# One PSUM product ahead of the second context transpose, 56 unread products ahead of the first inverse, one weight cast bound in the merge

## The chip, the cores and the metric

The kernel runs on one core of a Trainium2 chip. The metric is the time of one execution on the device, in microseconds (us). The engines are TensorE (PE in the rows, PEld for its weight loads), VectorE (DVE), ScalarE (ACT), GpSimd (POOL) and SyncE (SP), whose queue issues most DMAs.

## What is computed

One layer of a hybrid network over 512 latent tokens and 256 context tokens of width 1024, batch 1, in fp32. Cut to what matters here:

```
x   = ffn(x);  ctx = ffn(ctx)                       # half-step SwiGLU blocks with adaLN modulation
qa, ka, va, qkv, z, a, b, ga, gb = split(modulate(x)   @ w_in)   # and the same for ctx
o_a = neighbourhood_attention(qa, ka, va, ctx keys)
q, k, v = silu(conv(qkv)) ...                       # gated delta rule, 4 heads, two directions
per chunk:  T = inverse(I + tril(k k^T * decay * beta));  scan over chunks
o_b = rmsnorm(scan output) * silu(z)
y   = sigmoid(ga) * (o_a @ w_pa) + sigmoid(gb) * (o_b @ w_pb)    # the merge
x   = LN(alpha*x + gate * (y @ w_o));  x = ffn(x)
```

## The kernel before

**Products.** Every weight is cast into two fp32r parts, a rounded one (`wh`, on ScalarE) and the rest (`wl`, on VectorE), in `split`, and so is every activation (`uxh`, `uxl` for the latent tokens, `uch`, `ucl` for the context). A product of 128 weights by 512 tokens is three matmuls for each of 8 slices of the depth (`mm3k`, lines 190 to 192). A `Stream` loads weights by DMA (line 172) and casts them one or two tiles ahead of their use, into a few rotating buffers.

**Order.** The instructions of the whole program are put in order on each engine when the program is built, by a planner: it times them by its own estimates and takes, among those that it holds ready, the one that stands first in the code. On the chip each engine works through its queue in that order, and waits where an input is late. `tc.issue_after(x)` holds an instruction behind `x` in the queue of their engine.

**PSUM.** PSUM has eight banks of 128x512 fp32. The up and down products of the first block use the pool `pp` with one tag `ps` of eight tiles, handed out in rotation. The last users of that pool are the four `z` products, the transposes of the context tokens in `u2(fc, pp, "c", 0, ...)`, the first product of `units[0]` (the query of head 0) and the transposes of `u2(fc, pp, "c", 1, ...)`. A call of `u2` takes two tiles: TensorE writes four 128x128 transposes into each (line 146), ScalarE reads them into `u` (line 149), and `split` makes `uch` and `ucl` of that. Then the pool is closed, and its banks go to the pools `pm` (three tiles for products) and `pg` (five for transposes). The first tile of `pm` is the key product of head 0.

**Gram stage, inverse and scan.** The delta rule is done in three batches `bi` of chunks. `grams(bi)` loads the decays (`Dt<-gcd`), makes the Gram products (`pq`, line 857), scales them on VectorE (`Bt`, line 927, `At`, line 931) and stores them (`bd<-Bt`); `base_inverse` loads 32x32 diagonal blocks back (`Ltr`, `L`), inverts them row by row on VectorE (lines 954, 955) and stores them (`rd<-Xt`). `inverse` loads these (`T<-rd`, line 976), transposes them on VectorE (lines 978, 979), and joins them with small products into the tag `pi`, each read by VectorE or ScalarE before the next. `scan_step` uses the tag `pc` of two tiles. Behind each of these small products `turn` lets some pieces of the other projections (`fill_spill`, 6 matmuls each, tag `pm`) run on TensorE. The code says `step(grams(0))`, which includes the base inverse of the first batch, `base = grams(1)`, then `inv_of(0, 0)`, `step(base, 4)` and so on: the second base inverse on VectorE lies beside the first two inverses.

**Merge.** For each of 8 tiles `m` the loop fills the stream `wso` of `w_o` weights, makes the product with `w_pa` from the stream `ws` (`gated`), multiplies it by the gate (line 1333, VectorE), adds it to `yb` (line 1334, GpSimd) and splits the sum into `yh`, `yl`. The gates are loaded (`gt<-gad`) into two buffers. `wso` items 4 to 6 have buffers in a pool that opens right ahead of this loop. After it come the products with `w_o`, and in `finish2` the residual `xr<-x1d`, loaded from GpSimd's queue into memory that the merge has used, and a layer norm for each of four token tiles.

Of the kernel before, what the change touches and what calls it, by code (L numbers as in the profile page):

```python
# [10 lines left out]
F32 = mybir.dt.float32  # L11
F32R = mybir.dt.float32r
AF = mybir.ActivationFunctionType
ALU = mybir.AluOpType
# [4 lines left out]
P = 128  # L19
# [39 lines left out]
def body(ctx, tc, I, out, dbg=None):  # L59
    nc = tc.nc  # L60
    V, S, G, T = nc.vector, nc.scalar, nc.gpsimd, nc.tensor
    dbg = dbg or {}

    def pool(name, side="left", space=None):
        kw = dict(name=name, bufs=1, reuse_waits="tile")
        if space is not None:
            kw["space"] = space
        else:
            kw["side"] = side
        g = tc.tile_pool(**kw)  # L70
        st = ExitStack()
        p = st.enter_context(g)
        return p, st.close
# [3 lines left out]
    def tl(p, shape, tag, bufs=1, dt=F32):  # L77
        uid[0] += 1
        return p.tile(list(shape), dt, name=f"{tag}_{uid[0]}", tag=tag, bufs=bufs)
# [22 lines left out]
    marks = {}  # L102
# [29 lines left out]
    def split(src, hi, lo, behind=()):  # L132

        with tc.issue_after(behind[0]) if behind else nullcontext():
            S.copy(hi, src)  # L135
        with tc.issue_after(behind[1]) if behind else nullcontext():
            V.tensor_tensor(lo, src, hi.bitcast(F32), ALU.subtract)  # L137

    def to_u(tp, pp, xn, uh, ul, c0, scale, shift, tag="u32"):

        u32 = tl(tp, [P, KT, P], tag)
        for hb in range(2):
            ps = tl(pp, [P, 4, P], "ps", 8)
            for q in range(4):
                k = hb * 4 + q
                T.transpose(ps[:, q, :], xn[:, k * P:(k + 1) * P], ident)
            for q in range(4):
                k = hb * 4 + q
                S.activation(u32[:, k, :], ps[:, q, :], AF.Identity, bias=shift[:, k:k + 1], scale=scale[:, k:k + 1])
            ks = slice(hb * 4, hb * 4 + 4)  # L150
            split(u32[:, ks], uh[:, ks, c0:c0 + P], ul[:, ks, c0:c0 + P])
        return u32

    class Stream:
# [7 lines left out]
        def fill(self, n):  # L162
            while len(self.q) < n and self.i < len(self.srcs):
                src, p, bufs, rp, rb = self.srcs[self.i], self.wp, self.bufs, self.wp, self.bufs
                if isinstance(src, tuple):
                    if src[1] not in self.extra:
                        return
                    p, bufs, rp, rb = self.extra[src[1]]
                    src = src[0]
                c = src.shape[-1]  # L170
                raw = self.raw() if self.raw else tl(rp, [P, D], "wr", rb)
                nc.sync.dma_start(raw[:, 0:c], src)
                hi = tl(p, [P, D], "wh", bufs, F32R)
                lo = tl(p, [P, D], "wl", bufs, F32R)
                split(raw[:, 0:c], hi[:, 0:c], lo[:, 0:c], self.behind.get(self.i, ()))
                self.q.append((hi, lo))
                self.i += 1

# [9 lines left out]
    def mm3k(ps, wh, wl, uh, ul, k, nk=KT):  # L188
        a, b = wh[:, k * P:k * P + P], wl[:, k * P:k * P + P]
        T.matmul(ps, a, uh[:, k, :], start=(k == 0), stop=False)  # L190
        T.matmul(ps, a, ul[:, k, :], start=False, stop=False)  # L191
        T.matmul(ps, b, uh[:, k, :], start=False, stop=(k == nk - 1))  # L192

    def down(pp, ws, hs, ntt, kl, pre=(), between=None, after=None, pieces=0, post=(), n=None):

# [115 lines left out]
    def secs(col, s):  # L311
        return col[:, s * 8:s * 8 + 8]
# [7 lines left out]
    def raw1():  # L320
        raws[0] += 1
        k = raws[0] % (5 if more[0] else 3)
        return tl(more[0], [P, D], "wr", 2) if k > 2 else tl(wx, [P, D], "wr") if k == 0 else tl(wp, [P, D], "wr", WB)
# [5 lines left out]
    uxh = tl(up, [P, KT, NX], "uxh", 1, F32R)  # L329
# [35 lines left out]
    def order1():  # L365
        t = lambda fs: [I["up1"][2 * f + j] for f in fs for j in range(2)]
        dn = lambda a, b: rows(I["dn1"], range(a, b))
        o = t(range(F0, F1)) + t(range(F1)) + t(range(F1, HF)) + dn(0, HF) + dn(0, HF - 2)
        o += t(range(HF, NF)) + dn(HF, NF - 4)
        n = len(o)  # L370
        o += dn(HF, NF - KL1)
        o = [(w, "x") if j % 3 == 2 else w for j, w in enumerate(o)]
        return o[:n] + [(w, "tail") for w in dn(NF - 4, NF)] + o[n:]
# [56 lines left out]
    pp, close_pp = pool("pp1", space=PSUM)  # L430
    ws = Stream(wp, order1(), WB, 1)
# [3 lines left out]
    for t in range(2):  # L435
        raw = raw1()
# [76 lines left out]
    def u2(p, pp, kind, t, y):  # L513
        uh, ul, col = (uxh, uxl, colx) if kind == "x" else (uch, ucl, colc)
        to_u(p, pp, y, uh, ul, t * P, secs(col, 4), secs(col, 3))
# [8 lines left out]
    uxh = tl(ux, [P, KT, NX], "uxh", 1, F32R)  # L524
# [31 lines left out]
    src = [I["wab"] if n == "ab" else I["w" + n][m] if n in ("pa", "pb") else I["win"][WIN_IDX[(n, m)]] for n, m in order]  # L556
# [18 lines left out]
    ws = ws2  # L575
    names = iter(order)

    def win_w(name, m):
        assert next(names) == (name, m)
        return ws.get()  # L580
# [240 lines left out]
        units += [decay()] * (h == 2) + [unit_q(h), unit_k(h), unit_v(h), unit_kc(h), unit_vc(h)]  # L821
    u2(fc, pp, "c", 0, ys[0])
    next(units[0])
    u2(fc, pp, "c", 1, ys[1])
    close_fc()
    close_pp()
# [18 lines left out]
    pgq, close_pgq = pool("pgb", space=PSUM)  # L845
# [68 lines left out]
    def gram(p, s, bd, g):  # L914

        mats = mats_of(s)
        Dt = tl(gb_, [P, 4, P], "Dt", 2)
        nc.sync.dma_start(Dt[:], bass.AP(gcd.tensor, gcd.offset + (4 * s + 2 * p) * P, [[0, P], [24 * P, 2], [1, 2 * P]]))
        for m, (d, c, i) in enumerate(mats):
            msk = cst[:, (C_MF if d == 0 else C_MB):][:, 0:P]  # L920
            V.scalar_tensor_tensor(Dt[:, m], Dt[:, m], gcum[:, d, s, 2 * p + i:2 * p + i + 1], msk, op0=ALU.subtract, op1=ALU.add)
        S.activation(Dt[:], Dt[:], AF.Exp)
        Bt, At = tl(gq, [P, 4, P], "Bt", NBT), None
        for n, t in enumerate(products(p, s)):
            if n == 0:
                for m, (d, c, i) in enumerate(mats):
                    V.scalar_tensor_tensor(Bt[:, m], t[m] if s == 1 else t[:, m], beta[:, d, s, 2 * p + i:2 * p + i + 1], Dt[:, m], op0=ALU.mult, op1=ALU.mult)
                nc.sync.dma_start(bass.AP(bd.tensor, bd.offset + g * MSTR, [[P, P], [4 * MSTR, 4], [1, P]]), Bt[:])
            else:
                At = tl(gq, [P, 4, P], "At", NAT)  # L930
                V.tensor_tensor(At[:], t[:], Dt[:], ALU.mult)
        return Bt, At
# [190 lines left out]
    def grams(bi):  # L1123
        bd = tl(dp, [16 * MSTR], f"bd{bi}")[:]
        rds[bi] = tl(dp, [64, 1024], f"rd{bi}")[:]
        for j in (0, 2, 1, 3) if bi == 0 else range(4):
            res[(bi, j)] = gram(j % 2, 2 * bi + j // 2, bd, 2 * (j % 2) + j // 2)
        return base_inverse(bd, rds[bi])

    def step(gen, n=8):  # L1130
        for _ in range(n):
            next(gen, None)

    def inv_of(bi, st):
        inv[(bi, 2 * st)], inv[(bi, 2 * st + 1)] = inverse(bi, st, rds[bi], [res[(bi, 2 * st + p)][0] for p in range(2)])
# [6 lines left out]
        next(fills)  # L1142
    step(grams(0))
    base = grams(1)
    inv_of(0, 0)
    step(base, 4)
    inv_of(0, 1)
# [134 lines left out]
    def gated(name, gd, m, oh, ol):  # L1282
        wh, wl = win_w(name, m)
        gt = tl(np_, [P, NX], "gt", 2)
        nc.sync.dma_start(gt[:], gd[m])
        ps = tl(pm, [P, NX], *PMB)
        mm3(ps[:], wh, wl, oh, ol, 4)
        return gt, ps
# [15 lines left out]
    for m in range(4):  # L1304
        if m == 3:
# [5 lines left out]
            wso = Stream(wp, [(w, k) if k else w for w, k in zip(rows(I["w_o"], range(KT)), ("b", "b", "b", "b", "o", "o", "o", ""))], WB, 1)  # L1311
# [18 lines left out]
    for m in range(8):  # L1330
        wso.fill(min(4 + (m + 1) // 2, 7))
        gt, ps = gated("pa", gad, m, oah, oal)
        V.scalar_tensor_tensor(gt[:], gt[:], 1.0, ps[:], op0=ALU.add, op1=ALU.mult)
        G.tensor_tensor(yb[:, m], yb[:, m], gt[:], ALU.add)
        split(yb[:, m], yh[:, m], yl[:, m])
# [4 lines left out]
    pp, close_pp = pool("pp3", space=PSUM)  # L1340
# [4 lines left out]
    uxh = tl(up, [P, KT, NX], "uxh", 1, F32R)  # L1345
# [70 lines left out]
    src = [I["up2"][i] for i in range(2 * NH)]  # L1416
    ws = Stream(wp, [(w, key(j)) if key(j) else w for j, w in enumerate(src)], WB, 2)
# [134 lines left out]
    ws = Stream(wp, [(w, "d") if j % 6 > 1 else w for j, w in enumerate(rows(I["dn2"], range(NF)))], WB, 2)  # L1552
    ws.extra = {"d": (wd, 4, wp, WB)}
    raw = hs[NH:]
# [7 lines left out]
    banks, _ = down(pp, ws, hs, 4, KL2, between=between, pieces=PIECES, n=NF)  # L1562
    for t in range(4):
        h = tl(lp, [P, D], "h4", 2)
        n, m = (512, D) if t < 3 else (D // PIECES, 512)
# [125 lines left out]
```

## Time and profile before

| | |
|---|---|
| runs without a profile | 1529.4, 1525.82, 1529.38 us; median 1529.38 us |
| the profiled execution | 1530.66 us, span of its instructions 1528.8 us |
| mean granted TensorE clock | 0.988 of full speed |
| instructions | 23646, of them 9221 matmuls |

A timeline row reads: start, duration, engine, line, operation, output<-inputs, shapes, count, and in brackets the idle time of the engine just ahead of it and what ended that. Matmuls are pipelined: the duration of one is longer than the distance to the next start, and it is the distance that is paid. A row of windows gives for a stretch its length, then the busy time of each engine with the count of instructions, the granted TensorE clock, the share of DMA and GB/s.

### The profile page before, as it was taken

The numbers are of one execution on the slowest core, as the hardware profiler recorded it, in microseconds if no ns is written. First come the engines' busy times: TensorE is split into PE (matmuls) and PEld (weight loads), VectorE is DVE, ScalarE is ACT, GpSimd is POOL, SyncE is SP. The second block draws the span as 40 slices with busy tenths as digits, with TensorE's granted clock in tenths as the row PEclk, the third lists the DMA queues.
The fourth block names the chain that finished last, engine by engine and source line by source line (L and its number), as shares of the span: only waits on it lengthen the run. The fifth ranks groups of instructions, "written<-read, shape, count | busy, mean of one in ns | idle before, by whom it ended". The sixth has DMA issues, their size and how long they took to land.

```text
span 1528.8 us, 23646 instructions
## 1 busy us (share of the span) xinstructions
PE 1462.6 (96%) x9221; PEld 1258.7 (82%) x9221; DVE 1050.0 (69%) x1792; ACT 605.4 (40%) x1005; POOL 226.8 (15%) x224
## 2 busy tenths in 40 slices
PE   6999999999999999999996899999999999999997
PEld 4779988888888887889875778867678999998886
DVE  8765942597554587768777895576669699886426
ACT  5444221322222255546543444266416444344310
POOL 0000000000000011323301001366421022220001
PEclk9999999999999999999998999999999999999999
DMA  9665742667454334222476634283353143333422
GB/s 370 207 237 180 222 142 97 211 213 260 168 192 146 130 112 137 87 90 79 141 216 180 172 99 122 69 284 117 91 174 138 56 139 102 106 110 139 138 83 83
DMA packets 107586, 230.72 MB, mean 151 GB/s; under 512 B 34177, under 2 KB 47825, under 8 KB 107473
## 3 DMA queue, kind: packets, MB, share of 16 engines
q1 hardware_dynamic: 105312, 221.79, 44.7%
q10 hardware_dynamic: 1586, 5.32, 0.9%
q0 software_dynamic: 576, 2.10, 0.4%
q8 instruction: 72, 1.18, 0.3%
q14 instruction: 40, 0.33, 0.1%
HBM read 206.33 MB, written 22.85 MB: 150 GB/s over the span
## 4 chain that ended last, share of the span: by engine, by line
PE 76%; DVE 10%; DMA 7%; issue 3%; ACT 2%; POOL 2%; SPq 0%; DVEq 0%; ACTq 0%; POOLq 0%
PE ps L209 19%; PE ps L190 8%; PE ps L192 8%; PE ps L191 8%; PE pm L190 5%; PE pm L192 5%; PE pm L191 5%; PE pc L857 2%; PE ps L1478 2%; PE ps L1480 2%; PE ps L1479 2%; DVE wl L137 2%; PE po L1266 1%; DMA T<-rd 1%; PE pt L1255 1%
## 5 line engine op out<-in xcount | busy, mean ns | idle before, releaser
L137 DVE TENSOR_TENSOR wl<-wr,wh 128x1024 fp32r<-128x1024 f32 (+1 forms) x215 | 263.0, 1228 | 195.1 <-ACT wh L135 194.3
L135 ACT CAST wh<-wr 128x1024 fp32r<-128x1024 f32 (+1 forms) x215 | 217.8, 1018 | 333.4 <-PE ps L209 105.0
L192 PE MATMUL ps<-uxh,wl 128*128 128x512 f32 (+1 forms) x496 | 179.6, 363 | 2.2 <-DVE wl L137 2.2
L191 PE MATMUL ps<-uxl,wh 128*128 128x512 f32 (+1 forms) x496 | 179.3, 363 | 0.8 <-DVE uxl L137 0.8
L190 PE MATMUL ps<-uxh,wh 128*128 128x512 f32 (+1 forms) x496 | 179.6, 365 | 0.0
L279 DVE SCALAR_TENSOR_TENSOR adap<-wr,crow 128x1024 f32<-128x1024 f32 x112 | 136.8, 1221 | 38.5 <-DMA wr<-in_w_adaT_dram 37.1
L112 POOL TENSOR_TENSOR rs<-ve,mhalf 128x1 f32<-128x1 f32 (+2 forms) x46 | 50.4, 1099 | 744.6 <-DVE ve L108 735.4
L190 PE MATMUL pm<-uxh,wh 128*128 128x512 f32 x320 | 133.0, 416 | 4.1 <-ACT spill L609 2.1
L192 PE MATMUL pm<-uxh,wl 128*128 128x512 f32 x320 | 128.2, 401 | 0.7 <-DVE wl L137 0.7
L191 PE MATMUL pm<-uxl,wh 128*128 128x512 f32 x320 | 127.8, 399 | 0.0
L192 PEld LDWEIGHTS ps<-uxh,wl 128*128 128x128 f32 x496 | 93.7, 189 | 17.9 <-DVE wl L137 3.3
L191 PEld LDWEIGHTS ps<-uxl,wh 128*128 128x128 f32 x496 | 94.0, 189 | 14.9 <-DVE uxl L137 1.0
L190 PEld LDWEIGHTS ps<-uxh,wh 128*128 128x128 f32 x496 | 93.4, 189 | 14.3 <-issue 0.8
L190 PE MATMUL ps<-uch,wh 128*128 128x256 f32 x352 | 98.6, 280 | 0.0
L192 PE MATMUL ps<-uch,wl 128*128 128x256 f32 x352 | 98.3, 279 | 0.0
L191 PE MATMUL ps<-ucl,wh 128*128 128x256 f32 x352 | 98.2, 279 | 0.0
L209 PE MATMUL ps<-wh,hx 128*128 128x512 f32 x352 | 94.8, 389 | 0.0
L209 PEld LDWEIGHTS ps<-wh,hx 128*128 128x128 f32 x352 | 65.9, 188 | 13.6
L190 PEld LDWEIGHTS pm<-uxh,wh 128*128 128x128 f32 x320 | 61.6, 193 | 16.3 <-ACT spill L609 3.0
L192 PEld LDWEIGHTS pm<-uxh,wl 128*128 128x128 f32 x320 | 61.7, 193 | 14.8 <-DVE wl L137 1.5
L191 PEld LDWEIGHTS pm<-uxl,wh 128*128 128x128 f32 x320 | 61.6, 192 | 10.6
L190 PEld LDWEIGHTS ps<-uch,wh 128*128 128x128 f32 x352 | 66.1, 188 | 0.6
(411 smaller groups left out, 3438.7 us busy)
## 6 DMA issues: line engine op xcount, KB each, us to landing
wr<-in_w_adaT_dram SPq DMA_DIRECT2D x88, 512.0 KB, 4.7
wr<-in_up_dram SPq DMA_DIRECT2D x80, 512.0 KB, 4.2
wr<-in_dn_dram SPq DMA_DIRECT2D x58, 512.0 KB, 3.5
wr<-in_win_dram SPq DMA_DIRECT2D x52, 512.0 KB, 3.9
rb<-in_up_dram SPq DMA_DIRECT2D x18, 512.0 KB, 3.7
wr<-in_w_o_dram SPq DMA_DIRECT2D x8, 512.0 KB, 4.0
ac<-in_up_dram SPq DMA_DIRECT2D x6, 512.0 KB, 5.2
Dt<-gcd SPq DMA_DIRECT2D x12, 256.0 KB, 5.1
```

Of the source, the lines that this page charges most:

```text
L112: G.tensor_tensor(rs[:], ve[:], mhalf[:, 0:n], ALU.pow)
L135: S.copy(hi, src)
L137: V.tensor_tensor(lo, src, hi.bitcast(F32), ALU.subtract)
L190: T.matmul(ps, a, uh[:, k, :], start=(k == 0), stop=False)
L191: T.matmul(ps, a, ul[:, k, :], start=False, stop=False)
L192: T.matmul(ps, b, uh[:, k, :], start=False, stop=(k == nk - 1))
L209: T.matmul(banks[t][d][:, c0:c1], a[:, sl], b[:, d * 512 + c0:d * 512 + c1], start=first and j == 0, stop=last and j == 2)
L279: V.scalar_tensor_tensor(pr[:], raw[:], 1.0, crow, op0=ALU.mult, op1=ALU.mult, accum_out=col[:, c:c + 1])
L857: last[0] = T.matmul(*a, **k).ins
L1478: T.matmul(ps[:], a, uh[:, k], start=k == 0, stop=False)
L1479: T.matmul(ps[:], a, ul[:, k], start=False, stop=False)
L1480: T.matmul(ps[:], b, uh[:, k], start=False, stop=k == 3)
```

## The change

Three things are added. First, behind the last matmul of the query product of head 0, one matmul of 128 by 64 columns goes into a `ps` tile of its own; nothing reads it. Second, between `grams(1)` and `inv_of(0, 0)`, 56 matmuls of 128 by 512 columns go into one `pc` tile, queued behind the last matmul of the filling pieces; nothing reads them. Third, the cast of the sixth `w_o` tile (index 5), both parts, is held behind the cast of the tile that `ws` cast last at `m == 2`. `split` returns its two instructions for that, and `mm3k` marks its last matmul.

```diff
     def split(src, hi, lo, behind=()):
         with tc.issue_after(behind[0]) if behind else nullcontext():
-            S.copy(hi, src)
+            a = S.copy(hi, src).ins
         with tc.issue_after(behind[1]) if behind else nullcontext():
-            V.tensor_tensor(lo, src, hi.bitcast(F32), ALU.subtract)
+            b = V.tensor_tensor(lo, src, hi.bitcast(F32), ALU.subtract).ins
+        return a, b
...
-                split(raw[:, 0:c], hi[:, 0:c], lo[:, 0:c], self.behind.get(self.i, ()))
+                self.last = split(raw[:, 0:c], hi[:, 0:c], lo[:, 0:c], self.behind.get(self.i, ()))
...
-        T.matmul(ps, b, uh[:, k, :], start=False, stop=(k == nk - 1))
+        marks["mm"] = T.matmul(ps, b, uh[:, k, :], start=False, stop=(k == nk - 1)).ins
...
     next(units[0])
+    with tc.issue_after(marks["mm"]):
+        T.matmul(tl(pp, [P, 512], "ps", 8)[:, 0:64], uxh[:, 0, 0:P], uxh[:, 0, 0:64], start=True, stop=True)
     u2(fc, pp, "c", 1, ys[1])
...
     base = grams(1)
+    spare, ahead = tl(pgq, [P, 4, P], "pc", 2)[:].rearrange("p m c -> p (m c)"), marks["mm"]
+    for _ in range(56):
+        with tc.issue_after(ahead):
+            T.matmul(spare, uxh[:, 0, 0:P], uxh[:, 0, :], start=True, stop=True)
     inv_of(0, 0)
...
         gt, ps = gated("pa", gad, m, oah, oal)
+        if m == 2:
+            wso.behind[5] = ws.last
```

## Rows read from the trace of the kernel before

**Rows 1.** The page: shares of the chain that ended last
```profile
PE 76%; DVE 10%; DMA 7%; issue 3%; ACT 2%; POOL 2%; SPq 0%; DVEq 0%; ACTq 0%; POOLq 0%
```

**Rows 2.** Waits of TensorE: total us, times, longest us
```profile
PE pi L857 <- DMA T<-rd: 13.0, 2, 12.4
...
PE pi L857 <- DVE Y L1025: 3.5, 2, 2.8
...
PE pm L190 <- ACT u L149: 1.9, 1, 1.9
```

**Rows 3.** Timeline of TensorE around the pool change
```profile
607.60 1.03 PE L146 MATMUL ps<-ident,y 128*128 128x128 f32 x8
610.56 0.58 PE L190 MATMUL pm<-uxh,wh 128*128 128x512 f32 x1 [1.92 <-ACT u L149]
...
614.31 0.39 PE L190 MATMUL pm<-uxh,wh 128*128 128x512 f32 x1
```

**Rows 4.** Timelines of ScalarE and VectorE around the pool change
```profile
609.00 2.90 ACT L149 ACTIVATE u<-ps,colc 128x128 f32<-128x128 f32 x8
...
614.48 0.68 DVE L137 TENSOR_TENSOR ucl<-u,uch 128x512 fp32r<-128x512 f32 x1
```

**Rows 5.** One window from behind the pool change into the Gram stage
```profile
620.00:775.00 155.00, 155.00 (x960) 138.22 (x959) 113.95 (x196) 81.78 (x133) 44.67 (x45) 1.00 0.36 111
```

**Rows 6.** Timeline of TensorE at the end of the Gram stage and the first inverse
```profile
813.33 0.40 PE L191 MATMUL pm<-uxl,wh 128*128 128x512 f32 x1
...
818.32 0.39 PE L192 MATMUL pm<-uxh,wl 128*128 128x512 f32 x1
831.15 0.68 PE L857 MATMUL pi<-T,Bt 32*32 32x32 f32 x32 [12.44 <-DMA T<-rd]
...
834.62 0.65 PE L857 MATMUL pi<-Y,T 32*32 32x32 f32 x32
...
836.41 0.40 PE L190 MATMUL pm<-uxh,wh 128*128 128x512 f32 x1
...
838.57 0.45 PE L857 MATMUL pi<-T,Y 32*32 32x32 f32 x32
...
840.53 0.68 PE L857 MATMUL pi<-T,Bt 64*64 64x64 f32 x16
```

**Rows 7.** Windows of 5 us in the same stretch
```profile
830.00:835.00 5.00, 3.85 (x66) 2.75 (x70) 4.00 (x17) 2.26 (x5) 3.19 (x7) 0.50 0.25 75
...
840.00:845.00 5.00, 4.30 (x36) 3.07 (x36) 4.69 (x15) 3.46 (x7) 0.00 (x0) 1.00 0.00 1
```

**Rows 8.** Timeline of VectorE in the same stretch
```profile
830.83 0.31 DVE L978 STREAM_TRANSPOSE T<-T 128x128 f32<-128x128 f32 x1 [2.98 <-DMA T<-rd]
...
833.08 0.27 DVE L998 COPY Y<-pi 128x128 f32<-128x128 f32 x1
```

**Rows 9.** The chain that ended last, in that stretch
```profile
835.57 0.17 issue
```

**Rows 10.** Timelines of VectorE and GpSimd in the merge
```profile
1095.88 2.36 DVE L137 TENSOR_TENSOR wl<-wr,wh 128x1024 fp32r<-128x1024 f32 x2 [0.26 <-ACT wh L135]
1098.77 1.29 DVE L1333 SCALAR_TENSOR_TENSOR gt<-gt,pm 128x512 f32<-128x512 f32 x2 [0.53 <-PE pm L192]
...
1119.81 2.32 DVE L137 TENSOR_TENSOR wl<-wr,wh 128x1024 fp32r<-128x1024 f32 x1
...
1099.54 2.97 POOL L1334 TENSOR_TENSOR yb<-yb,gt 128x512 f32<-128x512 f32 x2 [9.30 <-DVE gt L1333]
...
1119.37 1.67 POOL L1334 TENSOR_TENSOR yb<-yb,gt 128x512 f32<-128x512 f32 x1 [2.89 <-DVE gt L1333]
```

**Rows 11.** The chain that ended last, in the merge and behind it
```profile
1104.83 0.50 issue
1105.33 0.68 DVE gt L1333
...
1107.79 3.26 DMA gt<-gad
```

## The prediction

> **What bounds the kernel now.** I read the shares of the chain that ended last first: TensorE holds 76% of it [rows 1], so most stages end with a product, and time is to be had only where TensorE stands still or runs slowly. The waits of TensorE come next [rows 2]. One is large, 12.4 us of an inverse product for its loaded blocks `T`; one of 1.9 us is for ScalarE's reads of PSUM. The two places are where the first two edits sit, so I read the timelines there. The third edit sits in the merge, where VectorE and GpSimd are on the chain.
>
> At the pool change the last eight transposes start at 607.60 and the first product of the new pool at 610.56, after 1.92 us without work, released when ScalarE had read the first four of the eight slices [rows 3, 4]. The nine matmuls from 610.56 to 614.31 take 3.75 us, 0.417 us each. The full-rate distance is in the Gram stage: 813.33 to 818.32 holds 22 steps, 4.99 / 22 = 0.227 us [rows 6]. So behind the wait the products went at about half rate. From 620 to 775 TensorE was busy for all 155 us at full clock [rows 5]: what is gained ahead of 620 stays gained up to there.
>
> At the end of the Gram stage the last product starts at 818.32 and the first inverse product at 831.15 [rows 6]. The granted clock from 830 to 835 is 0.50, the lower level of 1.2 GHz [rows 7]. In the same rows VectorE is busy 4.00 of 5 us, and 4.69 of 5 from 840 to 845, while TensorE has idle time again by then. TensorE later waits 3.5 us, in two waits, for VectorE's copies `Y` [rows 2]. So behind the gap it is VectorE, not TensorE, that sets the pace.
>
> **Edit 1, the product ahead of the second transpose.** It adds one matmul of 64 columns and one weight load. The eight transposes of 128 columns show 1.03 us together, 0.13 each [rows 3]; I take 0.1 us, between 0 and the 0.227 of a 512-column product. It has no reader, so nothing waits for it except the bank. What it does is turn the rotation: the bank that the new pool's first tile wants is then the added product's, and the first four transposes go one bank further. That follows from the wait itself, which ended when the first half was read. Removed is the wait of 1.92 us and, if the clock holds without it, 3.75 - 9 x 0.227 = 1.71 us of half rate. What is late next: the key product then ends at about 608.65 + 24 x 0.227 = 614.1, and the context product behind it needs the last part of `ucl`, done at 614.48 + 0.68 = 615.16 [rows 4]. That is a wait of 0 (the value product can stand in between) to 1.1 us; I take 0, since the context product begins with the slices that come first. Sum: -1.92 - 1.71 + 0.1 = -3.5 us. Bounds: -3.6, and -0.6 if the half rate stays and the full 1.1 us is paid (-1.92 + 0.2 + 1.1). No DMA and no other queue is touched.
>
> **Edit 2, the 56 products.** They add 56 x 0.227 = 12.7 us to TensorE's queue, and stand ahead of the first inverse's products, so those cannot start before they are through. They can begin where a next product would have, 818.32 + 0.23 = 818.55, and end at 831.27. The inverse began at 831.15. They fit with an overrun of 0.1 us; their cover is a wait that the products do not shorten, since `T` comes over VectorE, a store and a load. Without that cover they would cost 12.7 us. No read waits for them, and the `pc` tile they use is wanted again only in the scan. What they give is the clock. From 831.15 to 834.62 one group of 32 small products and six large ones took 3.47 us; the same from 838.57 to 840.53 took 1.96 us: 1.51 lost. From 834.62 to 836.41, a group and three large ones took 1.79 against 1.96 - 3 x 0.227 = 1.28: 0.51 lost [rows 6]. Together 2.0 us of TensorE time come back. But who waits for TensorE there? The first group was done by about 831.8, and VectorE copied `Y` only at 833.08, in its turn [rows 8]. On the chain the only piece that hangs on the slow products is 0.17 us ahead of a weight cast, whose ScalarE half waits for a buffer [rows 9]. I take -0.2 us with the 0.1 of overrun inside it; ends -2.0 and +0.1.
>
> By the Trainium skill, "TensorE: Matmul & The Clock Gate", section "What's actually happening", the throttled clock is the default and activity releases it, so products without a reader buy the full rate for what follows. The trace agrees as far as it goes: 0.50 behind the gap, 1.00 from 840 on [rows 7]. By that rule alone the edit would be worth the whole 2.0 us; it is the first rival below.
>
> **Edit 3, the bound cast.** In the trace two `w_o` casts run at 1095.88 on VectorE, 2.36 us for both, and are over before VectorE waits 0.53 us for the first merge product [rows 10]. Item 5 was one of those two by the order of the code, so it costs nothing where it is. Bound behind the cast of the fourth `w_pa` tile it falls between the first two gate products, over at 1098.77 + 1.29, and that of `m = 2` at 1105.33 [rows 10, 11]. Ahead of that third one the chain has 0.50 us of slack, and behind it hang GpSimd's add, which frees a gate buffer, and the load of a gate of 3.26 us [rows 11]. ScalarE's half is free: ScalarE idles there. No DMA moves: its load is long done, and the next `w_o` load waits for item 4's buffer. VectorE's half is 2.36 / 2 = 1.2 us alone; another cast of that shape took 2.32 us while GpSimd added [rows 10]. GpSimd adds from 1099.54 for 2.97 us, so the cast mostly falls behind that. I take 1.2 - 0.5 = +0.7 us; ends 0 (the planner puts it behind the gate product) and 2.3 - 0.5 = +1.8.
>
> The Trainium skill speaks against this edit: "SBUF — State Buffer", section "Who interferes with whom", says that a VectorE instruction with two SBUF inputs contends with a GpSimd instruction that reads SBUF. The rows above agree, 2.32 against 1.2. By that rule a cast moved into GpSimd's stretch costs 1.8, and the sum below would be -1.9 in place of -3.0.
>
> **Sum.** -3.5 - 0.2 + 0.7 = -3.0 us. Against the profiled execution, 1530.66 - 3.0 = 1527.7. That execution is 1.3 us above the median of the runs shown, 1529.38 (its span is 1528.8), so as a median I forecast 1526.4 us. 0.3% is 4.6 us, about what a measurement of this kernel can tell from no change. The likeliest case has a range of its own from 1529.4 - 3.6 - 0.2 = 1525.6 to 1529.4 - 0.6 + 0.1 + 1.8 = 1530.7.
>
> **Rivals.**
>
> *The clock is paid in full.* TensorE's 2.0 us reach the end, because the planner uses the earlier products to put VectorE's copies of the first inverse earlier, and the moved cast hides: -3.5 - 2.0 = -5.5, 1523.9 us. For it: 76% of the chain is TensorE. Against it: VectorE's busy share behind the gap and the 3.5 us that TensorE waits for `Y`.
>
> *The 56 products push the inverse back in the plan (slower).* The queues are drawn up from the planner's times. VectorE stood 2.98 us at the transposes of `T` [rows 8], so the plan had `T` at least that much earlier, and a gap of at most 12.6 - 3.0 = 9.6 us. 12.7 us of products overrun that plan by 3.1 us; if the planner counts each at the 0.39 of a record, 21.8 us, by 12.2. By that much more of the second base inverse then stands ahead of each `Y` in VectorE's queue. It decides once the overrun is larger than about 3.5 us, the waits for `Y` that TensorE bears now. Midway, 7.7 us, paid in full: -3.5 + 0.7 + 7.7 = +4.9, 1534.3 us. Against it: VectorE's work in the stretch is the same in any order, and the Gram results behind it would come sooner.
>
> *Edit 1 does not do what it says.* The new pool's first tile still falls on a bank that ScalarE reads: the wait stays, or lasts to the end of the second half, 611.90, 1.3 us later. Sum: 0.1 - 0.2 + 0.7 = +0.6, 1530.0 us, at worst 1531.3. Against it: one turn of the rotation is all that is needed, by the release after the first half.
>
> **How the numbers follow.** Likeliest 0.42, clock in full 0.30, pushed back 0.16, no turn 0.12. Below 1524.8 us (faster by over 0.3%) lies nearly all of the second case and a tenth of the likeliest from a planner that gains elsewhere: 0.36. Above 1534.0 lies most of the third and little else: 0.15. Between them 0.49. The range goes down to 1520, the second case with as much again of order luck, and up to 1535, just above the third; about 0.18 is left out. The case range of the likeliest, 1525.6 to 1530.7, stands beside it.
>
> **What the profile after would show.** Edit 1: no wait for ScalarE's `u` at the pool change, and 0.23 us between the products behind it. Edit 2: 56 products of 0.227 us, a wait for `T` under 1 us, a granted clock of 1.00 from 830 on, and still waits for `Y`, longer than 3.5 us, if VectorE is the bound. Edit 3: one 128x1024 cast fewer on VectorE ahead of 1098, and the gate product of `m = 2` about 0.7 us later behind its predecessor. The prediction is wrong if the planner's new order moves other stages: a new wait of more than 1 us outside these places would show it, or if the half rate at the pool change is not an effect of the wait.

## The result and the profile after

The changed kernel took 1535.52 us (median of 6 runs, 1531.86 to 1538.86), the kernel before 1528.84 (6 runs): a ratio of 1.0049, 95% interval 1.0036 to 1.0062. It is slower by 6.7 us, and the interval lies clear of 1, where 1526.4 us was forecast; the time lies 0.5 us above the range. The profiled execution took 1534.75 us, with a span of 1533.0.

Edit 1 shows as forecast. The timeline of TensorE at the pool change:

```profile
607.42 0.19 PE L827 MATMUL ps<-uxh 128*128 128x64 f32 x1
607.46 1.07 PE L147 MATMUL ps<-ident,y 128*128 128x128 f32 x8
608.28 0.48 PE L191 MATMUL pm<-uxh,wh 128*128 128x512 f32 x1
...
610.42 0.39 PE L191 MATMUL pm<-uxh,wh 128*128 128x512 f32 x1
```

The wait for ScalarE's `u` is gone [rows 3], and the nine products behind it go from 608.28 to 610.42, 2.14 us in place of 3.75.

Edit 2's products also run where they were expected. TensorE's timeline at the first inverse, then two windows (columns as in [rows 7]) and TensorE's waits (us in total, times, longest):

```profile
812.91 12.86 PE L1153 MATMUL pc<-uxh 128*128 128x512 f32 x56
828.67 0.48 PE L861 MATMUL pi<-T,Bt 32*32 32x32 f32 x32 [2.90 <-DMA T<-rd]
...
836.44 0.65 PE L861 MATMUL pi<-Y,T 32*32 32x32 f32 x32 [5.71 <-DVE Y L1002]
...
837.62 0.63 PE L192 MATMUL pm<-uxl,wh 128*128 128x512 f32 x1
838.04 0.63 PE L193 MATMUL pm<-uxh,wl 128*128 128x512 f32 x1
```
```profile
830.00:835.00 5.00, 0.74 (x4) 0.26 (x2) 4.55 (x15) 1.91 (x3) 2.96 (x6) 0.94 0.31 105
840.00:845.00 5.00, 5.00 (x62) 3.62 (x62) 3.86 (x9) 1.45 (x5) 0.00 (x0) 0.88 0.30 105
```
```profile
PE pi L861 <- DMA T<-rd: 5.7, 2, 2.9
PE pi L861 <- DVE Y L1002: 5.7, 1, 5.7
...
PE pi L861 <- DVE Y L1029: 3.0, 1, 3.0
```

The 56 products take 12.86 us inside the old wait, and the first inverse product starts 2.5 us earlier than in [rows 6]. The granted clock behind it is 0.94 in place of 0.50 [rows 7]. The wait that is left for `T` is 2.90 us, where less than 1 us was forecast: with edit 1 the products start at 812.91 and not at 818.55, but `T` comes only 2.5 us earlier. And the product on `Y`, at 834.62 before, now starts at 836.44: TensorE waits 5.71 us for VectorE's copy. Behind that wait the products stand 0.42 us apart, at half the rate: what the 56 products were to keep away is back. VectorE's timeline in those 5.71 us:

```profile
829.85 0.68 DVE L935 TENSOR_TENSOR At<-kq,Dt 128x512 f32<-128x512 f32 x1
830.45 0.21 DVE L959 TENSOR_REDUCE Xt<-bt 128x6 f32<-128x72 f32 x1
...
835.83 0.36 DVE L959 TENSOR_REDUCE Xt<-bt 128x10 f32<-128x200 f32 x1
836.11 0.28 DVE L1002 COPY Y<-pi 128x128 f32<-128x128 f32 x1
```

From 830.45 to 835.83 stand 17 steps of the next batch's base inverse, ahead of a copy whose product was done near 829; before, one such step stood between `At` and the copy at 833.08 [rows 8]. Two batches on, a base inverse is late again. The timelines of VectorE, of SP's queue and of TensorE at the third batch:

```profile
925.88 0.68 DVE L959 TENSOR_REDUCE Xt<-bt 128x16 f32<-128x512 f32 x1
...
941.53 0.61 DVE L983 STREAM_TRANSPOSE T<-T 128x128 f32<-128x128 f32 x2 [5.71 <-DMA T<-rd]
```
```profile
926.59 2.65 SPq L963 DMA_DIRECT2D rd<-Xt  x4
```
```profile
941.48 0.45 PE L861 MATMUL pi<-T,Bt 32*32 32x32 f32 x32 [2.82 <-DMA T<-rd]
```

The last step of the third base inverse is over at 926.6, only then does the store start, and VectorE and TensorE both stand for the loads behind it (before, TensorE waited 0.59 us here and VectorE 3.52). None of the three edits names this place.

In the merge, on VectorE's timeline, the bound cast shows: one cast of 128x1024 (1.23 us) stands ahead of the first gate products, where two stood [rows 10]:

```profile
1102.77 1.23 DVE L137 TENSOR_TENSOR wl<-wr,wh 128x1024 fp32r<-128x1024 f32 x1 [0.26 <-ACT wh L135]
1105.64 1.28 DVE L1345 SCALAR_TENSOR_TENSOR gt<-gt,pm 128x512 f32<-128x512 f32 x2 [1.65 <-PE pm L193]
1106.85 5.38 DVE L137 TENSOR_TENSOR wl<-wr,wh 128x512 fp32r<-128x512 f32 x4
```

A row names the shape of its first instruction only: the last two of these four are casts of 128x1024, 1.21 us each, from 1109.88 on, where before only one such cast stood between the gate products of `m` 1 and 2. So the bound one is among them.

### The profile page after: what moved, and what is told of

Same layout as the page of the kernel before. It is cut to its first block, busy times and chain, and to the rows that moved or that the text cites. A ratio compares the mean times of both kernels' runs of the same rounds, so it can differ in the third digit from the quotient of the medians.

```text
span 1533.0 us, 23757 instructions
## 1 busy us (share of the span) xinstructions
PE 1473.8 (96%) x9278; PEld 1269.9 (83%) x9278; DVE 1049.1 (68%) x1792; ACT 607.5 (40%) x1005; POOL 231.3 (15%) x224
## 4 chain that ended last, share of the span: by engine, by line
PE 80%; DVE 8%; DMA 5%; issue 2%; ACT 2%; SPq 1%; POOL 1%; DVEq 0%; ACTq 0%; POOLq 0%
PE ps L210 22%; PE ps L191 8%; PE ps L193 8%; PE ps L192 8%; PE pm L191 5%; PE pm L193 5%; PE pm L192 5%; PE ps L1491 3%; PE ps L1490 3%; PE ps L1492 3%; PE pc L861 3%; DVE wl L137 2%; DMA Dt<-gcd 1%; PE po L1275 1%; DMA T<-rd 1%
## 5 line engine op out<-in xcount | busy, mean ns | idle before, releaser
L135 ACT CAST wh<-wr 128x1024 fp32r<-128x1024 f32 (+1 forms) x215 | 218.0, 1018 | 342.2 <-PE ps L210 100.9
```

The costliest lines, as they stand in the source:

```text
L135: a = S.copy(hi, src).ins
```

## Experiments

Ratios are to the kernel before, timed side by side on the same chip in each of four series (e1 to e4, e5 to e8, e9 to e12, e13 to e16; its medians: 1527.76, 1526.39, 1526.32 and 1526.50 us), with 95% intervals. A ratio is estimated from all runs and is not the quotient of two medians; a share of time in the text is a difference of ratios.

**The edits apart (e1 to e4).** Each kernel is the kernel before with some of the edits: the product at the pool change alone (e1), the 56 products alone (e2), the bound cast alone (e3), the first two together (e4). The lines that are added to the kernel before (`marks["mm"]`, the last product of `mm3`, `spare`, `ahead` and the rest as in the change):

```diff
e1, e4:
+    with tc.issue_after(marks["mm"]):
+        T.matmul(tl(pp, [P, 512], "ps", 8)[:, 0:64], uxh[:, 0, 0:P], uxh[:, 0, 0:64], start=True, stop=True)
e2, e4:
+    for _ in range(56):
+        with tc.issue_after(ahead):
+            T.matmul(spare, uxh[:, 0, 0:P], uxh[:, 0, :], start=True, stop=True)
e3:
+        if m == 2:
+            wso.behind[5] = ws.last
```

e1: 

> Edit 1 alone. Every engine's queue is that of the kernel before, with one matmul more on TensorE, so only the bank of the transposes differs. If the turn of the rotation does what the trace of the changed kernel suggests, the wait of 1.9 us for ScalarE at the pool change and the half rate behind it go, and 3.5 us less arrive at the end: about 1525.3 us. The rival, that the 3.5 us are used up by VectorE's pace in the Gram and scan stages, gives 1528 to 1529.

e2: 

> Edit 2 alone, the 56 products. Theory of the order: VectorE's copy Y of the first inverse again stands behind ten more steps of the second base inverse, TensorE waits over 5 us for it, and the loss of about 4.5 us at the first inverse and some 3.5 us at the blocks of the third batch come without edits 1 and 3: 1535 to 1537 us. Rival, the bound cast of edit 3 is the cause: 1528 to 1530 us here.

e3: 

> Edit 3 alone, the bound cast. Theory of the order: it costs the 0.7 to 1.8 us of the prediction at the merge, 1529.5 to 1530.5 us. Rival, it is the cause of the slower time: 1534 us or more.

e4: 

> Edits 1 and 2 without the bound cast. Theory of the order: the sum of their own effects, 3.5 us less and 7 us more, 1532 to 1534 us. If the bound cast makes up for something that the products disturb in the merge, this one is slower than the whole change, over 1536 us; if the cast costs time, it is faster than the whole change, under 1534 us.

| | median us | ratio | interval |
|---|---|---|---|
| e1, edit 1 | 1524.92 | 0.9976 | 0.9963 to 0.9989 |
| e2, edit 2 | 1545.67 | 1.0122 | 1.0101 to 1.0142 |
| e3, edit 3 | 1525.18 | 0.9988 | 0.9973 to 1.0002 |
| e4, edits 1 and 2 | 1542.52 | 1.0093 | 1.0069 to 1.0118 |

Edit 1 gives 0.24%, 3.7 us (2.8 by the medians). Edit 2 is the loss, and a larger one than was expected or than the whole change has: by the medians 17.9 us alone, 17.6 us on top of edit 1 in e4. With the bound cast the loss is some 7 us smaller (the whole change against e4, from different series). In e4 TensorE's timeline in the merge has a wait that the whole change has not:

```profile
1109.91 0.50 PE L191 MATMUL pm<-oah,wh 128*128 128x512 f32 x1 [2.92 <-ACT wh L135]
```

ScalarE's casts, three of them from 1108.30, had waited 3.69 us there for a load of `w_o`. So edits 2 and 3 can't be priced apart from each other.

**Order or work (e5 to e8).** The 56 products do two things: they take TensorE's time, and they make the planner draw up other queues. To part these, a function at the end of the program ties every instruction of each engine behind the one that is to stand ahead of it, by edges of issue order only, from a table of the order of another kernel:

```diff
             body(ctx, tc, I, out)
+            queue_as(tc)
...
+    for e, order in ORDER.items():
+        own = [i for i in traced if i.engine == engines[e]]
+        for a, b in zip(order, order[1:]):
+            tc.add_manual_dep(own[b], own[a].name, no_sync, reason="order")
```

The 56 products are not in `traced`, and keep their place behind the Gram stage. The function moves the lines behind it by 18: L879 of these kernels is L861 of the changed one.

e5 is edits 1 and 3, planned freely; e6 is the same instructions in the changed kernel's order; e7 is edits 1 and 2 in e1's order; e8 is the whole change in e5's order. e5, as a diff of the changed kernel:

```diff
-    for _ in range(56):
-        with tc.issue_after(ahead):
-            T.matmul(spare, uxh[:, 0, 0:P], uxh[:, 0, :], start=True, stop=True)
```

e5: 

> Edits 1 and 3 without the 56 products. Order theory (the loss is the queue order that the plan makes when the 56 products are in it): no products, no such order, so this beats both kernels; the gains of the two single edits added to the kernel before (1527.76 - 2.84 - 2.58) give 1522.3 us, between 1521 and 1525. Rival (the bound cast only helps by repairing the merge order that the products disturb, and its own gain is chance): 1524.9, the time of edit 1 alone. A bound cast that costs 0.7 us, as forecast: 1525.6.

e6: 

> The 56 products are left out, and all five queues are bound to the order that they have in the changed kernel. Order theory: still slow, 1533 to 1537 us, with the copy of Y on VectorE near 836 us and the last gate product near 1127 us as in the changed kernel. Rival (the products cost by their own 12.9 us on TensorE, or by what they hold up behind them): without them the loss is gone, 1522 to 1526 us.

e7: 

> Edits 1 and 2: the 56 products are in, and all five queues are bound to the order that they have with edit 1 alone, so that the products stand in TensorE's queue at their place and nothing else moves. Order theory: the products run inside TensorE's 15.7 us wait and cost nothing; what the kept clock is worth behind them is all that is left, by the forecast's bounds 0.2 to 2.0 us: 1523 to 1524.8 us, against 1524.92 of edit 1 alone and 1542.52 of edits 1 and 2 in the plan's order. Rival (the products' own time costs): 1533 to 1543 us.

e8: 

> All three edits, with all five queues bound to the order that edits 1 and 3 have without the products. Order theory: the time of edits 1 and 3 (about 1522.3 us) less 0 to 2 us for the kept clock: 1520.5 to 1522.5. Rival (the products' own time costs): near the changed kernel, 1531 to 1536 us.

e5 took 1521.03 us, ratio 0.9963 (0.9949 to 0.9977); e6 1529.46, 1.0022 (1.0010 to 1.0034); e7 1525.33, 0.9992 (0.9981 to 1.0003); e8 1523.69, 0.9984 (0.9972 to 0.9995).

The order carries most of the loss, if less than was expected: e6 lies 0.59% above e5 (9.0 us) with not one of the products in it, and its timeline of TensorE has the late `Y`:

```profile
828.31 0.69 PE L879 MATMUL pi<-T,Bt 32*32 32x32 f32 x32 [15.61 <-DMA T<-rd]
836.10 0.65 PE L879 MATMUL pi<-Y,T 32*32 32x32 f32 x32 [4.23 <-DVE Y L1020]
```

With the products and without the order, in e8, there is no such wait:

```profile
812.91 12.86 PE L1171 MATMUL pc<-uxh 128*128 128x512 f32 x56
828.75 0.71 PE L879 MATMUL pi<-T,Bt 32*32 32x32 f32 x32 [2.99 <-DMA T<-rd]
832.17 0.45 PE L879 MATMUL pi<-Y,T 32*32 32x32 f32 x32
```

e5's VectorE shows what was swapped. One base step stands between `At` and the copy of `Y`, where the changed kernel has 17; and the third base inverse ends 6.7 us earlier:

```profile
830.44 0.68 DVE L935 TENSOR_TENSOR At<-kq,Dt 128x512 f32<-128x512 f32 x1
831.04 0.21 DVE L959 TENSOR_REDUCE Xt<-bt 128x6 f32<-128x72 f32 x1
831.17 0.27 DVE L1002 COPY Y<-pi 128x128 f32<-128x128 f32 x1
...
919.23 0.68 DVE L959 TENSOR_REDUCE Xt<-bt 128x16 f32<-128x512 f32 x1
```

Starts in the profiled executions, in us, carry the difference through the kernel:

| first start of | e5 | e6 | changed kernel |
|---|---|---|---|
| the first inverse product | 829.24 | 828.31 | 828.67 |
| the first product on `Y` | 832.72 | 836.10 | 836.44 |
| the first `pc<-r,Tt` of the scan | 882.13 | 885.58 | 885.88 |
| the scan's last transposes of `oacc` | 991.61 | 999.02 | 999.57 |
| the last gate product of the merge | 1116.25 | 1124.70 | 1127.08 |
| the first product on `t32h`, in the last block | 1216.80 | 1225.06 | 1227.53 |

Between e5 and e6, 3.4 us are lost at `Y`, 4.0 more up to the scan's end, 1.0 more up to the merge's. Profiles of the same two kernels taken again (e13 and e15 below) have 4.8, 5.3 and -1.3 at the same places: the losses up to the scan's end are in both, the 1.0 behind it is not. Behind the first `t32h` product the rest of the span takes 305.4 us in e5, 302.2 in e6 and 302.6 in e8, though no edit acts there: single profiled spans differ by 3 us, so small differences are read from the ratios.

The products are not free either: e8 lies 0.21% above e5 (3.2 us; the two intervals just touch), e7 0.16% above e1, from another series. The forecast bounds for them, given their order, were -2.0 to +0.1 us. Nor do they always keep the clock. In e7 the first inverse runs at the full rate behind them, and the first product on `Y` comes 2.3 us behind the first inverse product (e1: 3.5). In e8, whose rows stand above, it comes 3.4 us behind, as in e5, where nothing kept the clock. A window of e7, and the same of e8:

```profile
828.00:832.00 4.00, 3.82 (x48) 2.82 (x47) 3.76 (x14) 2.33 (x4) 3.44 (x7) 1.00 0.34 120
```
```profile
828.00:832.00 4.00, 3.25 (x38) 2.39 (x38) 3.44 (x15) 1.64 (x5) 2.62 (x6) 0.58 0.21 48
```

TensorE still waits for `T` behind the products, 2.55 us in e7 and 2.99 in e8, and behind that wait the granted clock is the lower one in e8 and not in e7. In e14, the kernel of e8 again, it is the lower one behind 2.76 us (0.57 in the same window); in the changed kernel it is not behind 2.90.

**Where the order loses (e9 to e11), and products of 2 columns (e12).** The tables mix the two orders: e5's everywhere but in one stretch, which is the changed kernel's. In e12, e5's order holds everywhere and the products are narrow:

```diff
-            T.matmul(spare, uxh[:, 0, 0:P], uxh[:, 0, :], start=True, stop=True)
+            T.matmul(spare[:, 0:2], uxh[:, 0, 0:P], uxh[:, 0, 0:2], start=True, stop=True)
```

e9: 

> Edits 1 and 3, no products; the queues are bound to the order without products but for VectorE's at the first inverses of the first two scan batches (86 places of its queue), which is the changed kernel's. If the loss at the first inverse lasts to the end: +3.4 us over edits 1 and 3 (the first right-hand side of the scan at 885.58 against 882.13 us in the two profiles), 1524.4 us. If the rest of the kernel has slack for it: 1521.0. If it alone carries the whole loss of the order: 1529.5.

e10: 

> As the last, but only the order around the third batch's inverses is the changed kernel's (67 places of VectorE's queue, some of TensorE, ScalarE, GpSimd and SP, whose loads of T stand later). If that part has its own loss: the last transpose of the scan was 7.4 us later with the new order, of which 3.4 were there before, so +4.0, 1525.0 us. If those 4.0 us only follow from what the first inverse left late: 1521.0 to 1522.

e11: 

> As the last, but only the order from the end of the scan through the attention and the merge is the changed kernel's. From the landmarks of the two profiles: +1 us (8.4 us at the end of the merge less 7.4 at the scan's last transpose), 1522.0 us. Rival (the merge's order is where the bound cast mattered, and so where most is lost): +4 or more, over 1525.

e12: 

> All three edits with the queues bound to the order without products, but each of the 56 products is 2 columns wide, so that they fill almost none of TensorE's wait. If the 2.7 us that the wide products cost in the old order (1523.69 against 1521.03) come from the instructions and their place in the PSUM ring: 1523.7. If they come from the wide products' work on TensorE: 1521.0.

e9 took 1525.34 us, ratio 0.9992 (0.9979 to 1.0004); e10 1526.00, 0.9995 (0.9984 to 1.0007); e11 1526.94, 1.0008 (0.9998 to 1.0018); e12 1522.57, 0.9973 (0.9961 to 0.9984). Against e5's 0.9963, each of the three stretches loses by itself: 0.29, 0.32 and 0.45%. That base is from another series; against e12, from the same one, they are 0.19, 0.22 and 0.35%. By either base the sum, 1.06 or 0.76%, is more than the 0.59% of all three together, which suggests that they are not terms of a sum; with intervals of 0.1% and more on each it isn't proved. e11's VectorE shows one way in which that can be:

```profile
935.96 0.31 DVE L1078 SCALAR_TENSOR_TENSOR r<-pc,neg,vtok 128x128 f32<-128x128 f32 x1
938.40 1.22 DVE L155 TENSOR_TENSOR wl<-wr,wh 128x1024 fp32r<-128x1024 f32 x1 [2.13 <-ACT wh L153]
939.54 0.86 DVE L1078 SCALAR_TENSOR_TENSOR r<-pc,neg,vtok 128x128 f32<-128x128 f32 x3
```

A weight cast stands between the first and the other three `r`, and waits 2.13 us for ScalarE's half. In the changed kernel the same cast stands there (942.29), but everything is so late by then that its input is ready, so that one loss can hide another. The landmarks had put 1.0 us on the late stretch; that reading was wrong.

e12 lies 0.10% above e5 and 0.11% below e8, inside the intervals of both, so it does not tell the products' instructions from their work.

**The pairs again (e13 to e16).** The kernels of e5, e8, e6 and the whole change, unaltered, timed again in one series, as e13 to e16.

e13: 

> Edits 1 and 3 without the products, a second time, as the base of the pairs: ratio to the kernel before 0.9963 in the first timing, 0.996 to 0.9975 here.

e14: 

> The same queues with the 56 wide products. If the products have a cost of their own: 0.2 per cent over e13, as in the first pair (3 us). If they are free where TensorE waits anyway: the same as e13 within 0.1 per cent. If the kept clock pays: under e13.

e15: 

> The changed kernel's queue order without the products: 0.5 to 0.6 per cent over e13 (8 to 9 us) if the order carries most of the loss.

e16: 

> The whole change: with a cost of the products' own, 0.2 to 0.3 per cent over e15 (3 to 4 us); without one, the same as e15 within 0.1 per cent.

| median us, ratio (interval) | without the 56 products | with them |
|---|---|---|
| e5's order | e13: 1518.74, 0.9947 (0.9934 to 0.9960) | e14: 1523.17, 0.9976 (0.9967 to 0.9986) |
| the changed kernel's order | e15: 1528.47, 1.0008 (0.9997 to 1.0018) | e16: 1531.64, 1.0032 (1.0021 to 1.0043) |

The order costs 0.61% without the products (9.3 us) and 0.56% with them; the products cost 0.29 and 0.24% (4.4 and 3.7 us) in either order. The first series gave 0.59, and 0.21 for the products in e5's order. So both costs are there, and the order's is the larger. The binding itself is not what costs: e14 and e15 are bound and e13 and e16 are not, so a cost of it would make each pair of differences unequal by twice its size, and they are unequal by 0.05% only, inside the noise.

Where the products' own 3 to 4 us go was not found. The three pairs of profiles in the order without products (e7 with e1, e8 with e5, e14 with e13) show a gain and a loss. From the first `pc<-r,Tt` to the scan's end the kernels with products took 108.0 to 109.2 us, those without 109.5 to 109.7: a gain near 1.0, though e9, without products, took 108.2 as well. From the first gate product of the merge to the last they took 27.5 to 29.2, those without 25.2 to 26.6: a loss near 2.3. One window of 4 us in the merge of e14, behind a wait of 2.41 us for a cast, and the one at the same place in e13, behind a wait of 1.89:

```profile
1115.00:1119.00 4.00, 4.00 (x11) 3.19 (x12) 3.48 (x4) 0.71 (x3) 1.65 (x1) 0.57 0.80 249
```
```profile
1109.00:1113.00 4.00, 4.00 (x19) 3.29 (x18) 3.15 (x4) 1.67 (x2) 1.39 (x1) 1.00 0.89 303
```

Eleven products against 19 in the same time: the granted clock fell to the lower level behind the wait in e14 and not in e13. All three kernels with products have such a stretch there, none of the three without, and in all three the wait ahead of it is longer (2.14 us for 1.18, 2.24 for 1.86, 2.41 for 1.89). It is not a rule: e6, without products but in the changed order, has such a stretch too, and the changed kernel, with them, has none. What connects products at 813 us with a wait at 1113 us no run shows.

**The version to keep.** e5, edits 1 and 3 without the products, beats both kernels: 0.9963 and, as e13, 0.9947 of the kernel before, 5.6 and 8.1 us.

## Why the prediction was wrong

**Edit 1** was right: -3.5 us forecast, -3.7 measured (e1; by the interval -5.7 to -1.7). The wait left and the half rate with it; the first products of the Gram stage start 3.7 us earlier in the changed kernel (747.21 for 750.87). How the lead reaches the end is less clear: in e1's profile it is 2.2 us at the first inverse product (828.96 for 831.15), 1.0 at the first `pc<-r,Tt` of the scan (882.90 for 883.88) and 4.2 at the last gate product of the merge (1115.07 for 1119.29), and single profiles of one kernel differ by as much.

**Edit 2** is the step that failed: "I take -0.2 us with the 0.1 of overrun inside it; ends -2.0 and +0.1." The cover was there: the products fit into the wait (12.86 us for the 12.7 forecast), and TensorE's first inverse product is not late. The cover was even mis-sized to the safe side: with edit 1 TensorE's wait for `T` is 15.66 us (e1), not 12.44, so that a wait is left behind the products, and the clock was granted behind it in the changed kernel and not in e8 and e14. What was priced at nothing is the new order of the other queues: 0.56 to 0.61%, 8.5 to 9.3 us (e13 to e16). The products' own 0.21 to 0.29%, 3 to 4 us, come on top, and their cause stays open. The mechanism of the order stood in the text as the second rival, at 0.16, with a price of +7.7 us, argued down by "VectorE's work in the stretch is the same in any order, and the Gram results behind it would come sooner". The work was the same. But the chain hangs on one copy in that work, and 16 more steps were put ahead of it. Two things of the rival were off as well. It placed the loss at the copies of `Y` beside the second base inverse alone; the order loses in three places (e9 to e11), and behind the first inverse the changed kernel's largest new wait is TensorE's 2.82 us for `T` at the third batch. And it took the 3.5 us that TensorE waits for `Y` now as slack that a push-back has to use up first; those waits are for the later copies (L1025 [rows 2]), and in the changed kernel 3.0 us of them stand beside the new 5.71. So it is in part luck that its price, 7.7 us, is near the order's 8 to 9. The forecast kept a sentence for this ("wrong if the planner's new order moves other stages"), and it is what happened; its chance was too small, and the upper end of the edit should have been the rival's.

By the Trainium skill, "TensorE: Matmul & The Clock Gate", section "What's actually happening", the default state is throttled and activity releases the throttle. The traces agree for the stretch right behind the products in the changed kernel (0.94 against 0.50) and in e7 (1.00 from 828 to 832), and in e8 and e14 the lower level is back behind the 3.0 and 2.8 us that TensorE still waits (0.58 and 0.57). Where the clock was kept it brought no gain in time: e7 has its first product on `Y` 1.2 us sooner behind the first inverse product than e1, and lies 0.16% above it (from another series). So the first rival, the clock paid in full at -2.0 us, fell too.

**Edit 3** was forecast at +0.7 us, 0.05%, and did not cost that: -0.12% alone (-0.27 to +0.02), and 0.13 and 0.29% below edit 1 in e5 and e13, from other series. A gain is likely by these, not proved. The part that was forecast is there: the merge, from its first gate product to its last, takes 26.6 and 26.4 us in e5 and e13 against 25.2 in e1. The 2.3 us of a cast beside GpSimd's add did not come true: in the changed kernel the bound cast took 1.21 us, behind the add, which was over at 1109.40. What was missed lies behind it. From the last gate product to the first `t32h` product the kernel before takes 104.2 us and e1 103.7, e3 100.6, e5 100.6 and e13 100.2. There TensorE waits for a copy of `y`, and in e1 runs slowly behind that wait; the window of e1, and the same of e5:

```profile
1182.00:1190.00 8.00, 8.00 (x58) 8.00 (x57) 1.95 (x4) 4.60 (x12) 0.00 (x0) 0.79 0.70 257
```
```profile
1182.00:1190.00 8.00, 8.00 (x71) 8.00 (x70) 2.66 (x5) 4.89 (x13) 0.00 (x0) 1.00 0.65 243
```

The wait is 2.02 us in e1 and 1.48 in e5; a second wait of 0.8 us, for the cast `uxl`, is in e1 and not in e5. Over the profiles, the clock fell behind waits for `y` of 2.14 us (before), 2.02 (e1) and 2.14 (e2), and not behind 1.92 (e3), 1.79 (e7) or shorter ones. That the shorter wait saves the clock is a reading of these rows; it was not tried by itself. Nor is it shown to be the bound cast's doing: e7, which has no bound cast and e1's order, takes 100.9 us for the same stretch at the full clock. With the products in the plan the bound cast seems worth more, 0.44% between e4 and the whole change (from different series), and the 2.92 us wait of e4's merge is not there.

**The third rival**, edit 1 without effect, is excluded by e1.

## What to carry to other kernels

Work that fits into a wait of its own engine can still cost when a planner sees it: compare every other engine's queue with the one before, and where it differs, price each copy or store that the chain hangs on by what now stands ahead of it. To part work from order, bind the queues to the old order with the new work in, and to the new order without it. An edit that costs a little where it sits may be paid back further on, so read on to the first landmark behind it that no edit moves. And work that is to keep the clock can leave a wait behind it in which the clock falls all the same (e8, e14): look at the granted clock there in more than one profile.

## What the runs showed of the hardware that was not expected

Products of 2 columns are not short, and the clock fell while they ran. In e12 the 56 took 8.45 us, 0.15 us each, against 0.23 for 512 columns. TensorE's timeline, and two windows of it:

```profile
812.61 8.45 PE L1171 MATMUL pc<-uxh 128*128 128x2 f32 x56
```
```profile
812.00:816.00 4.00, 4.00 (x36) 3.88 (x34) 2.98 (x4) 0.48 (x1) 0.00 (x0) 1.00 0.67 147
```
```profile
816.00:821.00 5.00, 5.00 (x27) 4.97 (x26) 0.64 (x3) 1.46 (x1) 0.00 (x0) 0.54 0.81 160
```

From 816 to 821 us TensorE shows no idle time, and the granted clock is 0.54, the lower level for most of it; with 512 columns in the same place, e8 is granted 1.00 from 815 to 828.

The lower level did not come behind equal waits alike. At the first inverse it came behind 2.76 us (e14) and not behind 2.90 (the changed kernel). In e5 TensorE waited 2.79 us up to 862.53 and 1.15 us up to 935.48, and windows of 4 us behind them (from 864 and from 936) show 0.57 and 0.59; in e13, the same kernel, it waited 2.80 us up to 859.94 and 1.16 up to 931.93, and no window of 4 us from 832 to 996 lies under 0.97. The eight timed executions of e5 lie up to 7.8 us apart (1517.83 to 1525.58).
